# One encoder layer on one core: where the plan puts the last attention head's neighbours, and how the last block of the final layer norm is cut up

## The chip, the cores and the metric

The kernel runs on one core of a Trainium2 chip. The metric is device time in microseconds (us) of one execution. A core has five engines with a queue each, which run in order and wait for each other through semaphores: TensorE (PE; its weight loads are shown as PEld), VectorE (DVE), ScalarE (ACT), GpSimd (POOL) and SyncE (SP). SP issues most DMAs; GpSimd issues those that add to what lies in the destination.

## The reference

One post-norm encoder layer over 512 tokens of width 1024, all in float32:

```python
proj = h @ w_in[l]                                   # q, k, v of both mixers
o_a = windowed_gqa_sink(qa, ka, va, a_sink[l])       # 16 q heads, 4 kv heads, |i-j| <= 128
o_b = dilated_mixture(qb, kb, vb)                    # 4 head slots, three dilations each
gates = jax.nn.sigmoid(h @ w_gate[l] + b_gate[l])
g_a, g_b = jnp.split(gates, N_BRANCH, axis=-1)
mixed = g_a * (o_a @ w_br_a[l]) + g_b * (o_b @ w_br_b[l])
y = mixed @ w_out[l]
h = layer_norm(DN_ALPHA * h + y, ln1_g[l], ln1_b[l])
f = (jax.nn.silu(h @ w_ff_gate[l]) * (h @ w_ff_up[l])) @ w_ff_down[l]
h = layer_norm(DN_ALPHA * h + f, ln2_g[l], ln2_b[l])
```

The layer norm takes mean and variance over the 1024 columns of a token, divides by sqrt(var + 1e-5), multiplies by a vector g and adds a vector b.

## The kernel before

**Products.** Every float32 operand is split into a high part (a copy rounded to fp32r) and a low part (the rest), and a product is three matmuls: high by high, high by low, low by high. So each weight tile of 128 x 512 (256 KB) costs a DMA, a copy on ScalarE or VectorE (L368, L370) and a subtraction on VectorE (`tt`, L539, or `split`, L394) before TensorE can use it. A 512-column matmul reads its columns in pairs (c, c + 256), so the 512 columns of a PSUM bank stand interleaved (`pairs`, `back`).

**The plan.** The program is not written in the order in which it runs. Each step adds operations to a list with `op`: its engine and estimated time, what it reads and writes, and a priority, which is the TensorE time of the plan so far plus an offset. `Program.run` then plays the list through with estimated times and issues, for each engine whenever it is free, the ready operation of the lowest priority. The real order of every queue comes out of this play. Limits stand for memory: `ws` staging tiles for loaded weights, `whl` tiles for their high and low parts, `gen` general tiles (`N_GEN` of them), `oa` tiles for fetched attention outputs. For a DMA the play adds up a common transfer time `moved` (1.0 times the cost of the DMA after the start) and lets it land 2.4 us later.

**ORDER.** The first half is a written list of steps. `P:a,b` computes two products of x at once with fewer multiplications (`pair_x`: seven products of 12 matmuls with 256 columns, L634 to L636; weights `A11`, `S1`, `A12`, `S3`, `A22`, of which `S1` and `S3` are each a load and a summing load on top). `g` is one gate's product alone (`gate`, `feat_k`, L518 to L520, 24 matmuls with 512 columns). `A0` to `A3` are the four windowed attention heads' groups (`unit_a`: scores L865 and L866, exponentials L1021, transposes L968, value products L1034 and L1035), `B0` to `B3` the dilated ones (`unit_b`, exponentials L1103). `R` turns rows (L707, L718, L806 are its copies from tile to tile by DMA), `V12` are two value projections (`token_values`, L939 to L941; eight tiles of weights, 96 matmuls of 512 columns), `L` lowers the limits from `N_WSA`, `N_WHLA` = 8, 16 to `N_WS`, `N_WHL` = 6, 12 once the last pair in front of it is done (`env["mark"]`). `O` fetches an attention output for the branch products (`fetch_oa`): a plain DMA (L1302) and a summing one from GpSimd (L1303), then a split (L1288). Gates of pairs are put away in DRAM (L1224) and fetched later.

**The final block.** `tok_major` ends both layer norms' products. In the second call (`fine` true), for each block of 128 tokens t, two PSUM banks `acc[t, 0]` and `acc[t, 1]` hold the two 512-column halves; for t = 2 and 3 the residual was copied into the banks first (`into`), so nothing need be added. For t = 3, the last, the work runs: the matmuls of half 0, its statistics (L1514), the matmuls of half 1, its statistics, their aggregation (L1517) to mean and variance, ScalarE's square root (L1519), (x - mean) * g on VectorE for each half (L1527), the reciprocal (L1530), and y * r + b on VectorE for half 0 whole and half 1 in two pieces of 256 columns (L1538), each followed by its store (`finish`, L1932).

Of the kernel before, what the change touches and what calls it, by code (L numbers as in the profile page):

```python
# [15 lines left out]
P = 128  # L16
# [44 lines left out]
UNITS = 2  # L61
SLOW = 340
SPIN = 4

CUTS = ((0, 128), (128, 256), (256, 512))
FIRST = {("k", 0): (-1000, -998.2, -997.2), ("q", 0): (-998.8, -998.1, -997.1), ("v", 0): (-998.7, -998, -997),
# [3 lines left out]
N_ALONG, N_WHL0 = 2, 24  # L70
ALONG_CUTS = ((0, 256), (256, 512))
FIRST.update({(0, 0): (-997.45, -996.97), (0, 1): (-996.65,), (1, 0): (-997.4, -996.96), (1, 1): (-996.45,)})
N_WS, N_WHL, N_ATT, N_GEN = 6, 12, 16, 60

# [4 lines left out]


ORDER = """
VA q1 A0 q2 q3 g X P:k1,q4 R A1 P:q5,g P:q6,q7 R A2 P:g,g A3 P:g,g P:Q00,K00 R P:Q01,K01 R L g V12 Q02 K02 R V0 B0 Q10 K10 R Q11 K11 R B1 O O Q12 K12 R O O B2 B3 O O O O g7
"""
FORMS = -60.0
XT_AFTER, LN_AFTER = ("B", 2), "b4"
STORE, OA, OA_SPLIT, OB_SPLIT, N_OA, N_XA = 0.0, -60.0, -140.0, -140, 4, 4
PACK = -60.0
BY_DMA = ()  # L90
AWAY = range(8, 16)
# [37 lines left out]
class Program:  # L129
# [67 lines left out]
    def run(self):  # L197
# [26 lines left out]
        while n_left:  # L224
# [11 lines left out]
            while progress:  # L236
                progress = False
                for e in engines:
# [26 lines left out]
                    o.eng = e  # L265
                    if e == SP:
                        end = now + (0.62 if 14 < now < SLOW else 0.47)
                        moved = max(moved, now + 0.9) + (1.5 if now < 9.5 else 1.0 if now < SLOW else 0.92) * cost
                        o.done = moved + (2.4 if 14 < now < SLOW else 0.87)
                    elif o.moves:  # L270
                        end = now + cost
                        moved = max(moved, end + 0.3) + (1.0 if 14 < now < SLOW else 0.92) * o.moves
                        o.done = moved + (0.87 if e == ACT else 6.2 if 330 < now < 420 else 3.2 if 14 < now < SLOW else 2.2)
                    else:
                        end = now + cost
                        o.done = end
# [50 lines left out]
def hybrid_layer(ctx: ExitStack, tc: tile.TileContext, wpack, xT, xtok, sink, bgate,  # L327
# [543 lines left out]
    def turned_values(u, nt, turn_by=0, done=None):  # L871

        src = []
        w = S // nt
        for i in range(2):
            ps = done
            if i or not done:
                ps = bank("dense")
                feat_x(ps, unit(u + i))
            t = slot()  # L880

            def evac(e, t=t, ps=ps):
# [9 lines left out]
            op(cp_alts(S, True, 0.3 if turn_by else 0.1)[:2 if turn_by else 1], evac, reads=[ps], writes=[t], prio=EV if i else NORM)  # L892
# [403 lines left out]
    def fetch_oa(k):  # L1296
# [5 lines left out]
        op([(SP, 0.73)], lambda e: nc.sync.dma_start(st.t, src(0)), reads=got, writes=[st], prio=OA)  # L1302
# [144 lines left out]
    xt = {(t, j): slot() for t in range(NR) for j in range(2)}  # L1447
    for t in range(NR):
        for j in range(2):
            load(xt[t, j], xtok[t, :, j * S:(j + 1) * S], after=env[XT_AFTER], prio=-30)  # L1450

    def ln_vectors(gsrc, bsrc, after):
        res = []
# [7 lines left out]
    def tok_major(nk, last, us_of, u0, g, b, finish, fine, alpha=ALPHA, between=None, into=(0, 1, 2), gates=()):  # L1461
# [4 lines left out]
        pr.hold = True  # L1466

        def kmm(k, t, j, c0, c1, us, wu):
            wh, wl = wu[j]
            ps = acc[t, j]  # L1470

            def go(e):
                a0, a1 = us[0].t[:, t * P:(t + 1) * P], us[1].t[:, t * P:(t + 1) * P]
                o = ps.t[:, c0:c1]
                mm(o, a0, pairs(wh.t[:, c0:c1]), start=(k == 0 and t not in into), stop=False, skip_group_check=True)  # L1475
                mm(o, a0, pairs(wl.t[:, c0:c1]), start=False, stop=False, skip_group_check=True)  # L1476
                mm(o, a1, pairs(wh.t[:, c0:c1]), start=False, stop=(k == nk - 1), skip_group_check=True)  # L1477
# [19 lines left out]
        for t in range(NR):  # L1497
            if not gates and t in into:
                preload(t)
            st = stats()  # L1500
            pieces = [(0, 0, S), (1, 0, S)]
            toks = []
            N2 = NORM - 10 * (fine and t == NR - 1)
            for n, (j, c0, c1) in enumerate(pieces):
                ps, z = acc[t, j], xt[t, j]
                for k, us, wu in res:
                    kmm(k, t, j, c0, c1, us, wu)
                toks.append(z)
# [5 lines left out]
                op([(DVE, dve(S))], lambda e, y=y, st=st, n=n: nc.vector.bn_stats(  # L1514
                    st.t[:, 6 * n:6 * n + 6], y.t), reads=[y], writes=[(st, n)], prio=N2)
            np_ = len(pieces)
            op([(DVE, 0.1)], lambda e, st=st, np_=np_: nc.vector.bn_aggr(st.t[:, 32:34], st.t[:, 0:6 * np_]),  # L1517
               reads=[(st, n) for n in range(np_)], writes=[(st, "a")], prio=N2)
            op([(ACT, 0.2)], lambda e, st=st: nc.scalar.activation(  # L1519
                st.t[:, 34:35], st.t[:, 33:34], AF.Sqrt, bias=eps.t[:, 0:1]), reads=[(st, "a"), eps],  # L1520
               writes=[(st, "s")], prio=N2, table="r")
            for (j, c0, c1), tok in zip(pieces, toks):
# [3 lines left out]
                op([(DVE, dve(S, extra=0.06))], lambda e, z=z, y=y, st=st, j=j, view_=view_:  # L1526
                   nc.vector.scalar_tensor_tensor(  # L1527
                       halves(z.t), view_(y.t), st.t[:, 32:33], halves(g[j].t), op0=ALU.subtract,
                       op1=ALU.mult), reads=[tok, y, (st, "a"), g[j]], writes=[tok], prio=N2)
            op([(DVE, 0.08)], lambda e, st=st: nc.vector.reciprocal(st.t[:, 35:36], st.t[:, 34:35]),  # L1530
               reads=[(st, "s")], writes=[(st, "r")], prio=N2)
            if fine and t == NR - 1:
                pieces = [(0, 0, S), (1, 0, S // 2), (1, S // 2, S)]
                toks = [xt[t, 0], (xt[t, 1], 0), (xt[t, 1], 1)]
            for (j, c0, c1), tok in zip(pieces, toks):
                z = xt[t, j]
                op([(DVE, dve(c1 - c0, extra=0.06))], lambda e, z=z, st=st, j=j, c0=c0, c1=c1:
                   nc.vector.scalar_tensor_tensor(  # L1538
                       z.t[:, c0:c1], z.t[:, c0:c1], st.t[:, 35:36], b[j].t[:, c0:c1], op0=ALU.mult,
                       op1=ALU.add), reads=[z, (st, "r"), b[j]], writes=[tok], prio=N2)  # L1540
                finish(t, j, c0, c1, tok)
            if between:
                between(t)
        pr.hold = False
# [496 lines left out]
```

## Time and profile before

| what | value |
|---|---|
| three runs | 730.40, 731.12, 732.73 us; median 731.12 |
| the profiled execution | 732.24 us, of which the span of the profile is 730.5 us |
| granted TensorE clock | 0.998 |
| TensorE busy | 719.8 us (99%) |
| VectorE, ScalarE, GpSimd busy | 656.0, 466.8, 136.8 us |
| DMA | 139.5 MB, mean 191 GB/s |

A group's row gives line, engine, operation, tiles (out<-in), shape and count, then busy us and the mean ns of one, then the idle time of the engine just before them and what ended it. A row of the time line gives start and duration in us; matmuls overlap in the pipeline, so the step from start to start, not the duration, is what one costs.

### The profile page before, as it was taken

Reading aid. Unit: us, or ns where it says so; the run is one execution under the profiler, and the core shown is the slowest. Engines: PE = TensorE matmul, PEld = TensorE weight load, DVE = VectorE, ACT = ScalarE, POOL = GpSimd, SP = SyncE. Lnnn points to the kernel's source line nnn. Section 1 sums busy time; section 2 is a strip of 40 time slices with the busy share of each in tenths; the row PEclk is TensorE's granted clock in tenths of the full one; section 3 lists DMA queues with packets and bytes.
Section 4 is the critical chain, followed back from the end, with each engine's and each line's share of the span. In section 5 each row is a group of like instructions: output and inputs, shape, how many; then the busy total and the mean of one; then the engine's idle time right before and its main releaser. Section 6 shows DMA issues by size and latency. Waiting matters only on the chain.

```text
span 730.5 us, 14312 instructions
## 1 busy us (share of the span) xinstructions
PE 719.8 (99%) x4731; PEld 665.6 (91%) x4731; DVE 656.0 (90%) x1404; ACT 466.8 (64%) x1069; POOL 136.8 (19%) x295
## 2 busy tenths in 40 slices
PE   9999999999999999999999999999999999999995
PEld 7889999898898888988888999999999999999984
DVE  6999999888888798898987999799999999899987
ACT  5667787777787575765451666656666556666821
POOL 0021211111010641530020021111102111113000
PEclk9999999999999999999999999999999999999999
DMA  8878789966759487765792389676888888979402
GB/s 262 286 162 204 178 231 238 276 173 170 191 142 227 130 214 209 243 186 173 214 208 68 97 270 226 160 185 155 210 247 214 204 200 225 257 190 198 100 30 86
DMA packets 87578, 139.51 MB, mean 191 GB/s; under 512 B 11088, under 2 KB 24016, under 8 KB 87504
## 3 DMA queue, kind: packets, MB, share of 16 engines
q1 hardware_dynamic: 74192, 114.61, 51.9%
q0 software_dynamic: 13040, 23.86, 20.2%
q8 instruction: 37, 0.61, 0.3%
q14 instruction: 37, 0.30, 0.1%
q10 hardware_dynamic: 272, 0.13, 0.1%
HBM read 114.18 MB, written 7.60 MB: 167 GB/s over the span
## 4 chain that ended last, share of the span: by engine, by line
PE 89%; DMA 6%; DVE 2%; SPq 2%; ACT 1%; issue 1%; DVEq 0%; ACTq 0%
PE ps L1686 9%; PE ps L1685 9%; PE ps L1687 9%; PE ps L518 7%; PE ps L519 7%; PE ps L520 7%; PE ps L1896 4%; PE ps L1898 4%; PE ps L1897 4%; PE ps L1476 3%; PE ps L1475 3%; PE ps L1477 3%; PE ps L968 3%; DMA sl<-wpack 2%; PE ps L634 2%; PE ps L636 2%
## 5 line engine op out<-in xcount | busy, mean ns | idle before, releaser
L368 ACT ACTIVATE sl<-sl 128x512 fp32r<-128x512 f32 (+3 forms) x413 | 226.3, 582 | 45.0 <-DVE sl L539 21.9
L539 DVE TENSOR_TENSOR sl<-sl,sl 128x512 fp32r<-128x512 f32 (+3 forms) x369 | 216.3, 622 | 6.5 <-ACT sl L368 2.9
L368 ACT ACTIVATE sl<-ps 128x256 f32<-128x256 f32 (+6 forms) x211 | 88.9, 443 | 92.0 <-PE ps L1687 56.8
L382 POOL DMA_DIRECT2D sl<-wpack x58 | 51.0, 879 | 345.0 <-DMA sl<-wpack 79.6
L518 PE MATMUL ps<-x,sl 128*128 128x512 f32 (+1 forms) x257 | 99.4, 387 | 0.1
L520 PE MATMUL ps<-x,sl 128*128 128x512 f32 (+1 forms) x257 | 97.3, 379 | 0.0
L1686 PE MATMUL ps<-sl,sl 128*128 128x256 f32 x352 | 96.8, 275 | 0.0
L1687 PE MATMUL ps<-sl,sl 128*128 128x256 f32 x352 | 96.8, 275 | 0.0
L1685 PE MATMUL ps<-sl,sl 128*128 128x256 f32 x352 | 96.8, 275 | 0.0
L519 PE MATMUL ps<-x,sl 128*128 128x512 f32 (+1 forms) x225 | 85.4, 380 | 0.0
L1685 PE MATMUL ps<-x,sl 128*128 128x256 f32 x264 | 72.6, 275 | 0.0
L1686 PE MATMUL ps<-x,sl 128*128 128x256 f32 x264 | 72.6, 275 | 0.0
L1687 PE MATMUL ps<-x,sl 128*128 128x256 f32 x264 | 72.6, 275 | 0.0
L394 DVE TENSOR_TENSOR sl<-sl,sl 128x512 fp32r<-128x512 f32 x98 | 65.6, 685 | 2.9 <-ACT sl L368 1.3
L1685 PEld LDWEIGHTS ps<-sl,sl 128*128 128x128 f32 x352 | 67.6, 192 | 0.1
L1686 PEld LDWEIGHTS ps<-sl,sl 128*128 128x128 f32 x352 | 67.6, 192 | 0.1
L1687 PEld LDWEIGHTS ps<-sl,sl 128*128 128x128 f32 x352 | 67.6, 192 | 0.0
L520 PEld LDWEIGHTS ps<-x,sl 128*128 128x128 f32 x257 | 48.8, 190 | 6.8
L518 PEld LDWEIGHTS ps<-x,sl 128*128 128x128 f32 x257 | 48.9, 190 | 6.1 <-ACT x L368 0.5
L1686 PEld LDWEIGHTS ps<-x,sl 128*128 128x128 f32 x264 | 50.6, 192 | 0.4
L1685 PEld LDWEIGHTS ps<-x,sl 128*128 128x128 f32 x264 | 50.6, 192 | 0.4
L1687 PEld LDWEIGHTS ps<-x,sl 128*128 128x128 f32 x264 | 50.7, 192 | 0.0
(174 smaller groups left out, 1818.1 us busy)
## 6 DMA issues: line engine op xcount, KB each, us to landing
sl<-wpack SPq DMA_DIRECT2D x248, 256.0 KB, 4.1
sl<-wpack POOLq DMA_DIRECT2D x58, 256.0 KB, 5.4
sl<-sl SPq DMA_DIRECT2D x110, 128.0 KB, 4.0
wf<-wpack SPq DMA_DIRECT2D x51, 256.0 KB, 5.1
wf<-wpack POOLq DMA_DIRECT2D x24, 256.0 KB, 6.3
oa<-sl SPq DMA_DIRECT2D x32, 128.0 KB, 3.7
sl<-sl SPq DMA_DIRECT2D x68, 32.0 KB, 2.4
sl<-oa SPq DMA_DIRECT2D x8, 256.0 KB, 3.9
```

The lines of the kernel that those rows point to most:

```text
L368: nc.scalar.activation(dst, src, AF.Copy)
L382: op([(POOL, 1.0)], lambda e: nc.gpsimd.dma_start(b.t, src2, accum_op=ALU.add), reads=[b], writes=[b], prio=prio, moves=1.65)
L394: op([(DVE, dve(S))], lambda e: nc.vector.tensor_tensor(l.t, src.t, f32(h.t), op=ALU.subtract), reads=[src, h], writes=[l], prio=prio, abs ...
L518: mm(o, a, x0, start=(k == 0 and begins), stop=False, skip_group_check=split)
L519: mm(o, a, x1, start=False, stop=False, skip_group_check=split)
L520: mm(o, b, x0, start=False, stop=(k == nk - 1), skip_group_check=split)
L539: op([(DVE, dve(w))], lambda e: nc.vector.tensor_tensor(dst(), x(), y(), op=o), reads=reads, writes=writes, prio=prio)
L1685: mm(o, wh, pairs(bh[k]()), start=(first and k == 0), stop=False, skip_group_check=True)
L1686: mm(o, wh, pairs(bl[k]()), start=False, stop=False, skip_group_check=True)
L1687: mm(o, wl, pairs(bh[k]()), start=False, stop=(k == 3), skip_group_check=True)
L1896: mm(ps.t, x0, pairs(w[0].t), start=(first and m == 0), stop=False, skip_group_check=True)
L1897: mm(ps.t, x0, pairs(w[1].t), start=False, stop=False, skip_group_check=True)
```

## The change

In `ORDER` the plain gate `g` that stood after `L` moves to directly behind `A3`, in front of the gate pair `P:g,g`; `L` moves from behind the pair `P:Q01,K01` to in front of the pair `P:Q00,K00`; and `V12` moves from behind both of these pairs to between them. In the play, a DMA between 90 and 165 us takes `RATE` = 1.7 times its cost, and `N_GEN` becomes 62. Each `fetch_oa` may be issued only after the exponentials of `B1` (and all before them). `LATE`, `VAL`, `XT_AFTER` and `OB_SPLIT` are new names or forms for values that stay the same.

In the final block of 128 tokens, half 1 is computed in two pieces of 256 PSUM columns, each with all its matmuls (24 of 256 columns for 12 of 512), and statistics are taken in four pieces of 256. Because of the interleaving, PSUM's first 256 columns are not the output's first 256; the second normalising step reads every other column. Output columns 256 to 511 of half 1 are normalised by ScalarE (x * r - mean * r, with a new small product on VectorE for mean * r), and multiplied by g and increased by b on GpSimd; VectorE does the rest. There are four stores of 256 columns, and the one behind GpSimd is the last.

```diff
+LATE = 2.4
+RATE = 1.7
...
-N_WS, N_WHL, N_ATT, N_GEN = 6, 12, 16, 60
+N_WS, N_WHL, N_ATT, N_GEN = 6, 12, 16, 62
...
-VA q1 A0 q2 q3 g X P:k1,q4 R A1 P:q5,g P:q6,q7 R A2 P:g,g A3 P:g,g P:Q00,K00 R P:Q01,K01 R L g V12 Q02 K02 R V0 B0 Q10 K10 R Q11 K11 R B1 O O Q12 K12 R O O B2 B3 O O O O g7
+VA q1 A0 q2 q3 g X P:k1,q4 R A1 P:q5,g P:q6,q7 R A2 P:g,g A3 g P:g,g L P:Q00,K00 R V12 P:Q01,K01 R Q02 K02 R V0 B0 Q10 K10 R Q11 K11 R B1 O O Q12 K12 R O O B2 B3 O O O O g7
...
-XT_AFTER, LN_AFTER = ("B", 2), "b4"
-STORE, OA, OA_SPLIT, OB_SPLIT, N_OA, N_XA = 0.0, -60.0, -140.0, -140, 4, 4
+SPREAD = True
+VAL = -100.0
+OA_AFTER = (1, 1, 1, 1, 1, 1, 1, 1)
+XT_AFTER, LN_AFTER = [('B', 2), ('B', 2), ('B', 2), ('B', 2)], "b4"
+STORE, OA, OA_SPLIT, OB_SPLIT, N_OA, N_XA = 0.0, -60.0, -140.0, -140.0, 4, 4
...
-                        moved = max(moved, now + 0.9) + (1.5 if now < 9.5 else 1.0 if now < SLOW else 0.92) * cost
-                        o.done = moved + (2.4 if 14 < now < SLOW else 0.87)
+                        moved = max(moved, now + 0.9) + (1.5 if now < 9.5 else RATE if 90 < now < 165 else 1.0 if now < SLOW else 0.92) * cost
+                        o.done = moved + (LATE if 95 < now < 150 else 2.4 if 14 < now < SLOW else 0.87)
...
-        op([(SP, 0.73)], lambda e: nc.sync.dma_start(st.t, src(0)), reads=got, writes=[st], prio=OA)
+        op([(SP, 0.73)], lambda e: nc.sync.dma_start(st.t, src(0)), reads=got, writes=[st], prio=OA, after=env["B", OA_AFTER[k]])
...
+            cut = c1 - c0 < S
...
-                mm(o, a0, pairs(wh.t[:, c0:c1]), start=(k == 0 and t not in into), stop=False, skip_group_check=True)
-                mm(o, a0, pairs(wl.t[:, c0:c1]), start=False, stop=False, skip_group_check=True)
-                mm(o, a1, pairs(wh.t[:, c0:c1]), start=False, stop=(k == nk - 1), skip_group_check=True)
-
-            op([(PE, 3 * pe(c1 - c0))], go, reads=[us[0].tok, us[1], wh, wl], writes=[ps])
+                w0, w1 = (pairs(w.t)[:, c0 // 2:c1 // 2] for w in (wh, wl))
+                mm(o, a0, w0, start=(k == 0 and t not in into), stop=False, skip_group_check=True)
+                mm(o, a0, w1, start=False, stop=False, skip_group_check=True)
+                mm(o, a1, w0, start=False, stop=(k == nk - 1), skip_group_check=True)
+
+            op([(PE, 3 * pe(c1 - c0))], go, reads=[us[0].tok, us[1], wh, wl] + ([ps] if cut else []),
+               writes=[(ps, c0) if cut else ps])
...
-            pieces = [(0, 0, S), (1, 0, S)]
+            ends = fine and t == NR - 1
+            pieces = [(0, 0, S // 2), (0, S // 2, S), (1, 0, S // 2), (1, S // 2, S)] if ends else [(0, 0, S), (1, 0, S)]
...
-                for k, us, wu in res:
-                    kmm(k, t, j, c0, c1, us, wu)
-                toks.append(z)
+                cut = (ps, c0) if ends and j else ps
+                if j or not ends:
+                    for k, us, wu in res:
+                        kmm(k, t, j, c0, c1, us, wu)
+                elif n == 0:
+                    for k, us, wu in res:
+                        kmm(k, t, j, 0, S, us, wu)
+                if c0 == 0:
+                    toks.append(z)
...
+                if ends and j and SPREAD:
+                    op([(DVE, dve(S // 2, extra=0.06))], lambda e, z=z, y=y, st=st, j=j: nc.vector.scalar_tensor_tensor(
+                        z.t[:, 0:256], back(y.t)[:, 0], st.t[:, 32:33], g[j].t[:, 0:256], op0=ALU.subtract,
+                        op1=ALU.mult), reads=[tok, (y, 0), (st, "a"), g[j]], writes=[(tok, 0)], prio=N2)
+                    continue
...
+                    z, ps, c = xt[t, 1], acc[t, 1], slice(S // 2, S)
+                    op([(DVE, 0.08)], lambda e, st=st: nc.vector.scalar_tensor_tensor(
+                        st.t[:, 36:37], st.t[:, 32:33], -1.0, st.t[:, 35:36], op0=ALU.mult, op1=ALU.mult),
+                       reads=[(st, "a"), (st, "r")], writes=[(st, "m")], prio=N2)
+                    op([(ACT, act(S // 2))], lambda e, st=st, z=z, ps=ps, c=c: nc.scalar.activation(
+                        z.t[:, c], back(ps.t)[:, 1], AF.Identity, scale=st.t[:, 35:36], bias=st.t[:, 36:37]),
+                       reads=[(st, "m"), ps, z], writes=[toks[2]], prio=N2)
+                    for x, o in ((g, ALU.mult), (b, ALU.add)):
+                        op([(POOL, 0.5)], lambda e, z=z, x=x, o=o, c=c: nc.gpsimd.tensor_tensor(
+                            z.t[:, c], z.t[:, c], x[1].t[:, c], op=o), reads=[toks[2], x[1]], writes=[toks[2]], prio=N2)
+                    pieces = [(1, 0, S // 2), (0, 0, S // 2), (0, S // 2, S)]
+                    toks = [toks[1], (xt[t, 0], 0), (xt[t, 0], 1), toks[2]]
...
+            if ends and SPREAD:
+                finish(t, 1, S // 2, S, toks[3])
```

More of the change, by code (lines that the diff above doesn't have):

```diff
@@ L890, in evac @@
                         copy(e, d, s)
-            op(cp_alts(S, True, 0.3 if turn_by else 0.1)[:2 if turn_by else 1], evac, reads=[ps], writes=[t], prio=EV if i else NORM)
+            op(cp_alts(S, True, 0.3 if turn_by else 0.1)[:2 if turn_by else 1], evac, reads=[ps], writes=[t], prio=VAL if i else NORM)
             src.append(t)
@@ L1449, in hybrid_layer @@
         for j in range(2):
-            load(xt[t, j], xtok[t, :, j * S:(j + 1) * S], after=env[XT_AFTER], prio=-30)
+            load(xt[t, j], xtok[t, :, j * S:(j + 1) * S], after=env[XT_AFTER[t]], prio=-30)
     def ln_vectors(gsrc, bsrc, after):
@@ L1513, in tok_major @@
                 y = z if t not in into else ps
-                op([(DVE, dve(S))], lambda e, y=y, st=st, n=n: nc.vector.bn_stats(
-                    st.t[:, 6 * n:6 * n + 6], y.t), reads=[y], writes=[(st, n)], prio=N2)
+                op([(DVE, dve(c1 - c0))], lambda e, y=y, st=st, n=n, c0=c0, c1=c1: nc.vector.bn_stats(
+                    st.t[:, 6 * n:6 * n + 6], y.t[:, c0:c1]), reads=[cut if t in into else y], writes=[(st, n)], prio=N2)
             np_ = len(pieces)
@@ L1521, in tok_major @@
                writes=[(st, "s")], prio=N2, table="r")
-            for (j, c0, c1), tok in zip(pieces, toks):
+            for j, tok in enumerate(toks):
                 z, ps = xt[t, j], acc[t, j]
                 y = z if t not in into else ps
+                if ends and j and SPREAD:
[3 more added lines that the diff above has]
+                    continue
                 view_ = halves if t not in into else back
@@ L1528, in tok_major @@
                        halves(z.t), view_(y.t), st.t[:, 32:33], halves(g[j].t), op0=ALU.subtract,
-                       op1=ALU.mult), reads=[tok, y, (st, "a"), g[j]], writes=[tok], prio=N2)
+                       op1=ALU.mult), reads=[tok, y, (st, "a"), g[j]], writes=[tok], prio=N2 + (ends and SPREAD and 1))
             op([(DVE, 0.08)], lambda e, st=st: nc.vector.reciprocal(st.t[:, 35:36], st.t[:, 34:35]),
                reads=[(st, "s")], writes=[(st, "r")], prio=N2)
-            if fine and t == NR - 1:
+            pieces = [(0, 0, S), (1, 0, S)]
+            if ends:
                 pieces = [(0, 0, S), (1, 0, S // 2), (1, S // 2, S)]
                 toks = [xt[t, 0], (xt[t, 1], 0), (xt[t, 1], 1)]
+                if SPREAD:
+                    z, ps, c = xt[t, 1], acc[t, 1], slice(S // 2, S)
[10 more added lines that the diff above has]
+                    toks = [toks[1], (xt[t, 0], 0), (xt[t, 0], 1), toks[2]]
             for (j, c0, c1), tok in zip(pieces, toks):
@@ L1539, in tok_major @@
                        z.t[:, c0:c1], z.t[:, c0:c1], st.t[:, 35:36], b[j].t[:, c0:c1], op0=ALU.mult,
-                       op1=ALU.add), reads=[z, (st, "r"), b[j]], writes=[tok], prio=N2)
+                       op1=ALU.add), reads=[z, tok, (st, "r"), b[j]], writes=[tok], prio=N2)
                 finish(t, j, c0, c1, tok)
+            if ends and SPREAD:
+                finish(t, 1, S // 2, S, toks[3])
             if between:
```

## The prediction

> **What bounds the kernel now.** I read the page first, then the busy time by stretches of 20 us, then TensorE's groups and the waits in the one stretch that stands out, then the time line of the end.
>
> ```profile
> PE 719.8 (99%) x4731; PEld 665.6 (91%) x4731; DVE 656.0 (90%) x1404; ACT 466.8 (64%) x1069; POOL 136.8 (19%) x295
> ```
>
> TensorE is busy for 719.8 of 730.5 us. So nothing can be gained by speeding another engine up, only where TensorE stands still. The stretches say where that is (the columns are the window, its length, busy us of PE, PEld, DVE, ACT and POOL with their instructions, the clock, the DMA share and GB/s):
>
> ```profile
> 120.00:140.00 20.00, 18.37 (x147) 16.98 (x145) 16.45 (x40) 14.79 (x39) 2.90 (x9) 1.00 0.99 283
> ...
> 160.00:180.00 20.00, 20.00 (x111) 18.01 (x110) 16.81 (x49) 15.42 (x41) 2.83 (x9) 1.00 0.66 177
> ...
> 420.00:440.00 20.00, 20.00 (x182) 20.00 (x181) 19.43 (x38) 13.77 (x28) 4.98 (x6) 1.00 0.88 261
> ```
>
> In 120 to 140 us TensorE lacks 1.6 us by busy time, and at the same moment the 16 DMA engines are full (share 0.99). Twenty microseconds later the share is 0.66. But a matmul's row overlaps its neighbours, so busy time hides short stalls. Counting is stricter. The row at 420 us holds nothing but 256-column matmuls and fits 182 of them into 20.00 us: 0.11 us each at full pace. TensorE's groups within 120 to 140 us:
>
> ```profile
> L634 PE MATMUL ps<-sl,sl 128*128 128x256 f32 x21 | 5.9, 283 | 0.2 <-ACT sl L642 0.2
> L635 PE MATMUL ps<-sl,sl 128*128 128x256 f32 x20 | 5.5, 275 | 0.0
> L636 PE MATMUL ps<-sl,sl 128*128 128x256 f32 x20 | 5.5, 275 | 0.0
> L634 PE MATMUL ps<-x,sl 128*128 128x256 f32 x18 | 5.0, 279 | 0.0
> L635 PE MATMUL ps<-x,sl 128*128 128x256 f32 x18 | 5.0, 275 | 0.0
> L636 PE MATMUL ps<-x,sl 128*128 128x256 f32 x18 | 5.0, 275 | 0.0
> L968 PE MATMUL ps<-ident,sl 128*128 128x128 f32 x16 | 2.6, 287 | 0.2 <-ACT sl L956 0.2
> L865 PE MATMUL ps<-sl,sl 128*128 128x384 f32 x6 | 2.0, 328 | 0.0
> L866 PE MATMUL ps<-sl,sl 128*128 128x384 f32 x6 | 2.0, 326 | 0.0
> L1035 PE MATMUL ps<-sl,sl 128*128 128x512 f32 x2 | 1.0, 483 | 1.2 <-DVE sl L973 1.1
> L1034 PE MATMUL ps<-sl,sl 128*128 128x512 f32 x2 | 0.8, 382 | 0.0
> ```
>
> 115 matmuls of 256 columns and 16 transposes at 0.11 us are 14.4 us, the 12 of 384 columns at one and a half times that 2.0, the four of 512 at twice that 0.9: 17.2 us of work in 20 us. So **2.8 us are lost in this stretch**. The largest loss lies between these two:
>
> ```profile
> 132.76 0.38 PE L1034 MATMUL ps<-sl,sl 128*128 128x512 f32 x1
> 134.26 0.48 PE L1035 MATMUL ps<-sl,sl 128*128 128x512 f32 x1 [1.11 <-DVE sl L973]
> ```
>
> The second should start about 0.22 us after the first and starts 1.50 us after it. It is the second half of an attention head's value product, and waits for VectorE's low part of the probabilities. What VectorE and ScalarE waited for themselves in 120 to 142 us:
>
> ```profile
> ACT sl L368 <- DMA gz<-sl: 2.1, 1, 2.1
> ACT sl L368 <- DMA sl<-sl: 1.5, 1, 1.5
> ACT sl L642 <- DMA sl<-sl: 1.2, 1, 1.2
> ```
> ```profile
> DVE sl L539 <- DMA sl<-sl: 2.1, 2, 1.8
> ```
>
> So the stall is a queue's: a copy or a split stands at the head of ScalarE's or VectorE's queue, waiting for a transfer that the plan had expected earlier, and the attention head's work, ready, stands behind it.
>
> **The change part by part.** *The order and the plan's constants.* Nothing is added to TensorE here. A weight-saving pair is 84 matmuls of 256 columns, 84 x 0.11 = 9.2 us, and takes 7 tiles of 256 KB: 0.19 MB per us. A plain gate is 24 matmuls of 512 columns, 5.2 us for 2 tiles, and V12 is 96, 20.7 us for 8 tiles: 0.10 MB per us each. Before, the last four pairs stand in one row and the gate and V12 after them; now the gate goes in front of the second gate pair and V12 between the last two pairs, so the heavy stretch is broken twice by work that needs half as much. The plan's RATE makes transfers 1.7 times as long between 90 and 165 us, so work that needs one is put later in the queues of ScalarE and VectorE, behind attention work that is ready. Both act on exactly the wait above. The fetches of attention outputs also leave the stretch:
>
> ```profile
> L1302 SPq DMA_DIRECT2D sl<-oa x8: 357/400/544, 136.0 to 244.7; - x8
> ```
> ```profile
> 268.83 0.50 ACT L1103 ACTIVATE sl<-sl,st 128x256 f32<-128x256 f32 x1
> ```
> ```profile
> 310.17 0.38 PE L518 MATMUL ps<-sl,sl 128*128 128x512 f32 x1
> 310.38 0.38 PE L519 MATMUL ps<-sl,sl 128*128 128x512 f32 x1
> ```
> ```profile
> sl<-wpack SPq DMA_DIRECT2D x248, 256.0 KB, 4.1
> sl<-wpack POOLq DMA_DIRECT2D x58, 256.0 KB, 5.4
> ```
>
> The first two of the eight (the first at 136.0 us), each with a summing transfer on GpSimd's queue behind it, go at the crowded time. Now all eight stand behind the exponentials of the second dilated head, which end at about 269 us (second row). They move past everything that SP and GpSimd issue until then, and the summing ones come among GpSimd's exchange copies of the dilated heads. Four buffers make two rounds of 4.1 + 5.4 = 9.5 us, so they have landed by about 288 us. The branch products that need them start at 310 us (third rows): some 20 us of dense products hide the move, and I cost it at nothing. Were that cover gone, TensorE would wait up to one round, 9.5 us. The constants that repeat their old value (LATE, VAL, XT_AFTER, OB_SPLIT) cost nothing, and two more general tiles (N_GEN) only allow more. I take the stall as gone: **-2.8 us**, ends 0 and -2.8. The transfers named above are then next to come late, elsewhere in the same stage.
>
> *The final block.* The end now:
>
> ```profile
> 722.64 0.38 PE L1477 MATMUL ps<-sl,sl 128*128 128x512 f32 x1
> 723.06 0.70 DVE L1514 BATCH_NORM_STATS2 st<-ps 128x6 f32<-128x512 f32 x1 [0.68 <-PE ps L1477]
> 723.79 0.21 DVE L1517 BATCH_NORM_AGGREGATE st<-st 128x2 f32<-128x12 f32 x1
> 724.04 0.29 ACT L1519 ACTIVATE st<-st,eps 128x1 f32<-128x1 f32 x1 [4.89 <-DVE st L1517]
> 724.04 1.41 DVE L1527 SCALAR_TENSOR_TENSOR sl<-ps,st,sl 128x512 f32<-128x512 f32 x2
> 725.37 0.15 DVE L1530 RECIPROCAL st<-st 128x1 f32<-128x1 f32 x1
> 725.55 1.54 DVE L1538 SCALAR_TENSOR_TENSOR sl<-sl,st,sl 128x512 f32<-128x512 f32 x3
> ```
>
> From 723.02 to 727.09 us only VectorE works; then come the last store and 3.4 us up to the span's end, which stay. Back to back a 512-wide VectorE pass is 1.41 / 2 = 0.70 us and a 256-wide one (1.54 - 0.70) / 2 = 0.42.
> - TensorE: 24 matmuls of 256 columns for 12 of 512, 24 x 0.11 = 2.64 against 12 x 0.21 (the step between the two rows at 310 us) = 2.52: +0.1 us.
> - The last statistics cover 256 columns: -0.28 us. But the first piece's statistics read the PSUM bank that the second piece's matmuls write. In the plan VectorE is busy with the block before, so that read falls among the second piece's products. If it holds them, TensorE stands for one pass and two hand-overs of 0.04 us (723.02 to 723.06): 0.5 us. If other columns of a bank may be written meanwhile, it costs 0. The row nearest is L634's wait for ScalarE's evacuation of its bank in the groups above (0.2 us idle); it shows the hold, though for the same columns. I take +0.45 us, ends 0 and 0.6.
> - The Trainium skill, "PSUM — Partial Sum Buffer", section "PSUM bank collisions raise a hardware error", says that accesses should be guarded by bank and quadrant, not by address. By that rule the term would be 0.5 us, by a guard on columns 0; no row here shows two engines on one bank at different columns.
> - Normalising takes 724.04 to 727.09 = 3.05 us now. Afterwards VectorE does 0.42 + 0.70 + 0.10 (reciprocal, the part that shows) + 0.15 (the new mean-times-scale, as a reciprocal) = 1.37 us, then ScalarE's pass over 256 columns, then GpSimd's product and sum one after the other; VectorE's own three 256-wide passes end earlier. Prices:
>
> ```profile
> L956 ACT ACTIVATE sl<-sl,st 128x256 f32<-128x256 f32 x37 | 16.4, 496 | 1.7 <-DVE st L1024 1.5
> ```
> ```profile
> L1113 POOL COPY st<-st 32x2 f32<-32x2 f32 x64 | 19.0, 297 | 7.6 <-ACT sl L1079 5.1
> ```
> ```profile
> L1056 POOL MEMSET sl<- 128x64 f32 x4 | 0.6, 153 | 4.1 <-DMA sl<-sl 3.4 <-PE ps L1034 0.7
> ```
>
> ScalarE's nearest pass has one column operand and takes 0.50 us; with two I take 0.55. No row has GpSimd combine two tiles. A copy of next to nothing takes 0.30 us, and a write of 64 columns without an input 0.15, so at most 2.4 ns a column. The low end for 256 columns is 0.30 us, the copy's fixed part alone; the high end is 0.30 + 256 x 2.4 ns = 0.92. I take the middle, 0.6 us, for each of the two, and 0.04 us for each of three hand-overs. Sum: 1.37 + 0.55 + 1.2 + 0.12 = 3.24 us, +0.2 against now, ends -0.4 and +0.85.
> - The Trainium skill, "GPSIMD Engine Reference", section 3.1, gives 2.6 cycles per element at 1.2 GHz for a two-input product, so 0.55 us for 256 columns and, by an estimate, some 0.7 with the start of the instruction; this term would then be +0.4 us. No run so far shows it.
>
> The block together: 0.1 + 0.45 - 0.28 + 0.2 = **+0.5 us** (ends -0.6 and +1.3). Splitting the work does not shorten the end, because the new chain of three engines is as long as the one it replaces.
>
> **The sum.** The profiled execution took 732.24 us, 730.5 of them its span; it lies 1.1 us above the median of the runs, 731.12. 732.24 - 2.8 + 0.5 = 729.9 us on its scale, **728.8 us** on the scale of the median: 0.32% faster. Measurements of this kernel tell about 0.3%, 2.2 us, from no change, so the forecast stands just beyond that bound, and a third of the stall staying would bring it inside.
>
> **The rivals.**
> *The stall only shrinks or moves.* The bytes and transfers stay the same in number, and a plan that errs by a microsecond on one landing makes the next stall. For it: outside this stretch TensorE is full already, so a re-planned stage can only lose. Against it: the rows at 160 us show the DMA engines with a third of their time free a moment later, to be had for the taking. With half of the 2.8 us left, and 0.5 to 1.3 at the end: 731.1 - 1.4 + 0.5 (to 1.3) = 730.2 to 731.0 us, no change that can be told.
>
> *Slower: the weight buffers run short.* The step L now comes before the last two pairs, not after them. It cuts the staging tiles from 8 to 6 and the split ones from 16 to 12. A pair uses 5 staging tiles in 9.2 us, 1.85 us each, so six tiles look 11.1 us ahead and eight 14.8. Two of the five are summed by two transfers one behind the other, 4.1 + 5.4 = 9.5 us at the median over the kernel. At 9.5 they are in time. The rival decides from 11.1 us on, 17% above the median, which transfers in a full stage can pass. At 12.1 us each of four summed tiles comes 1.0 us late, and each drags 0.7 us of split on VectorE behind it (0.70 us for 512 columns): 4 x 1.7 = 6.8 us, less what attention fills, which I put at half: 3.4. If the head of the queue is held in this way the old stall stays as well: 731.1 + 3.4 + 0.5 = 735.0 us. For it: at 120 to 140 us the DMA share is 0.99. Against it: V12 now stands between the two pairs and takes half the bytes per us, and the plan with RATE at 1.7 assumes late landings.
>
> *The end costs more, or the change does less than it says.* If the order settles as forecast but the end takes +1.3 us, 729.6 us; if GpSimd is quick and the bank is not held, 727.7. If the plan that comes out has nearly the same queue order around 130 us, the stall is untouched and only the end counts: 731.6 us.
>
> **How the numbers follow.** The forecast (stall gone, the end up to somewhat dearer) gets 0.52 for being faster by over 0.3%: the waits name the mechanism, and three parts of the change act on it (the order, RATE, the later fetches). No change within 0.3% gets 0.20: the shrunken stall, the untouched plan, the dear end. Slower by over 0.3% gets 0.28: the buffers, and other losses in stages that are full now. The range runs from 727.5 (stall gone and the end quick) to 735.5 (just beyond the buffers' case, 735.0). The forecast's own range is 727.5 to 729.6.
>
> **What would show it.** Right: 120 to 140 us with TensorE at 20.00 us, no 1 us wait of L1035 for VectorE, DMA share below 0.95 there, the first fetch of the attention outputs after 260 us. At the end: a GpSimd product and sum of 256 columns as the last work, the last store about 0.5 us later after the last matmul's old place than now, and a gap among the second piece's matmuls of some 0.45 us if the bank is held. Wrong: TensorE waiting for ScalarE's or VectorE's splits in the last two pairs (buffers), or a new wait anywhere between 160 and 350 us, where there is none now; GpSimd's passes far from 0.6 us would spoil the end's sum.

## The result and the profile after

The changed kernel takes **734.58 us** (median of 6 runs, 733.65 to 735.53), the kernel before in the same session 731.02 us (729.5 to 732.73). The ratio is 1.0044, with a 95% interval of 1.0031 to 1.0056: slower by 3.2 us by this ratio (the two medians lie 3.6 us apart), beyond the 0.3% that can be told. The profiled execution took 735.53 us, 733.8 of them its span, which is 3.3 us longer than the span before. I had forecast 2.3 us less.

The page's first row, in which TensorE's busy time has hardly changed:

```profile
PE 719.9 (98%) x4743; PEld 666.3 (91%) x4743; DVE 654.8 (89%) x1403; ACT 470.1 (64%) x1074; POOL 137.3 (19%) x297
```

So the time came from places where TensorE stands, or from after its last matmul. Busy time by stretches of the changed kernel (same columns as before):

```profile
120.00:140.00 20.00, 20.00 (x166) 19.61 (x165) 18.47 (x43) 16.69 (x40) 1.86 (x8) 1.00 0.62 172
...
310.00:320.00 10.00, 8.96 (x37) 6.33 (x36) 5.60 (x17) 5.25 (x13) 8.76 (x35) 1.00 1.06 321
```

The old stall is gone: 166 matmuls where there were 147, the DMA share down from 0.99 to 0.62. Counted by starts, each against the usual step of a matmul of its shape, TensorE had lost 3.3 us between 120 and 160 us and now loses nothing there. But a new stall stands at 311 to 320 us. That count gives 2.7 us from 300 to 330 us, 2.4 of them in the stall itself, and nothing was lost there before. The waits of the changed kernel from 310 to 320 us (total us, times, longest):

```profile
ACT x L373 <- DMA sl<-oa: 4.3, 4, 2.1
DVE sl L1293 <- ACT x L373: 2.9, 3, 1.7
PEld ps L524 <- DVE sl L1293: 1.9, 4, 0.6
...
PE ps L524 <- DVE sl L1293: 0.6, 3, 0.2
```

This reads upwards from TensorE: the product waits for VectorE's low part, that for ScalarE's rounding, and that for a fetch of the attention outputs (`sl<-oa`), one of the transfers that the change made later. And the time line of the end:

```profile
721.10 0.28 PE L1485 MATMUL ps<-sl,sl 128*128 128x256 f32 x1
721.42 0.43 DVE L1530 BATCH_NORM_STATS2 st<-ps 128x6 f32<-128x256 f32 x1
...
721.90 0.38 PE L1483 MATMUL ps<-sl,sl 128*128 128x256 f32 x1 [0.53 <-DVE st L1530]
...
722.88 0.43 DVE L1530 BATCH_NORM_STATS2 st<-ps 128x6 f32<-128x256 f32 x1 [1.03 <-PE ps L1485]
723.34 0.26 DVE L1533 BATCH_NORM_AGGREGATE st<-st 128x2 f32<-128x24 f32 x1
...
723.64 0.48 DVE L1542 SCALAR_TENSOR_TENSOR sl<-ps,st,sl 128x256 f32<-128x256 f32 x1
724.04 0.74 DVE L1548 SCALAR_TENSOR_TENSOR sl<-ps,st,sl 128x512 f32<-128x512 f32 x1
724.70 0.15 DVE L1551 RECIPROCAL st<-st 128x1 f32<-128x1 f32 x1
724.89 0.16 DVE L1560 SCALAR_TENSOR_TENSOR st<-st 128x1 f32<-128x1 f32 x1
...
725.14 0.56 ACT L1563 ACTIVATE sl<-ps,st 128x256 f32<-128x256 f32 x1 [1.21 <-DVE st L1560]
725.86 1.76 POOL L1567 TENSOR_TENSOR sl<-sl,sl 128x256 f32<-128x256 f32 x2 [39.12 <-ACT sl L1563]
```

GpSimd's two passes end at 727.62 us, and 6.1 us later the span, where 3.4 had followed the last VectorE pass before. The chain that ended last says with what it closes (start, us, what):

```profile
725.86 0.96 POOL sl L1567
726.82 0.04 issue
726.86 0.76 POOLq L2074
```

L2074 is the end of the program. Every engine closes its queue there with an instruction called a drain, and then all of them meet in a barrier, that is, each waits until the others have come. The source view of that line after, then of the same line (L2036) before; the columns are shortest, median and longest in ns, then the first and last start in us:

```profile
L2074 POOLq EVENT_SEMAPHORE  x4: 17/17/17, 733.0 to 733.7; - x4
L2074 POOLq DRAIN  x3: 51/93/6107, 726.9 to 733.5; - x3
L2074 SPq DRAIN  x3: 7/7/7, 729.9 to 733.2; - x3
```

The same line before:

```profile
L2036 POOLq EVENT_SEMAPHORE  x4: 17/17/17, 729.7 to 730.4; - x4
L2036 POOLq DRAIN  x3: 51/102/9037, 686.6 to 730.2; - x3
L2036 SPq DRAIN  x3: 7/7/13, 729.6 to 729.9; - x3
```

After, GpSimd's first drain starts with its last pass, at 726.86 us, and lasts 6.11 us, to 732.97, which is 5.35 us behind the pass's end. SyncE has seen all stores land at 729.9 us, and the barrier's first step waits until 733.0. Before, GpSimd's drain lay at 686.6 to 695.6 us, where nobody waited for it; the barrier followed SyncE by 0.1 us.

### The profile page after: what moved, and what is told of

It is laid out like the page before. It is cut to its first block, busy times and chain, and to the rows that moved or that the text cites. A ratio compares the mean times of both kernels' runs of the same rounds, so it can differ in the third digit from the quotient of the medians.

```text
span 733.8 us, 14304 instructions
## 1 busy us (share of the span) xinstructions
PE 719.9 (98%) x4743; PEld 666.3 (91%) x4743; DVE 654.8 (89%) x1403; ACT 470.1 (64%) x1074; POOL 137.3 (19%) x297
## 4 chain that ended last, share of the span: by engine, by line
PE 91%; DMA 4%; POOL 1%; SPq 1%; DVE 1%; issue 0%; ACT 0%; POOLq 0%; ACTq 0%
PE ps L1724 9%; PE ps L1723 9%; PE ps L1725 9%; PE ps L524 7%; PE ps L523 7%; PE ps L525 7%; PE ps L1934 4%; PE ps L1936 4%; PE ps L1935 4%; DMA sl<-wpack 4%; PE ps L641 3%; PE ps L640 3%; PE ps L639 3%; PE ps L1483 3%; PE ps L973 3%; PE ps L1485 3%
## 5 line engine op out<-in xcount | busy, mean ns | idle before, releaser
L373 ACT ACTIVATE sl<-ps 128x256 f32<-128x256 f32 (+5 forms) x210 | 88.5, 441 | 93.3 <-PE ps L1725 56.9
```

Source lines behind the costliest of these rows:

```text
L373: nc.scalar.activation(dst, src, AF.Copy)
```

## The experiments

The theory after this comparison: the new end costs mostly GpSimd's closing drain, 3.05 us between SyncE at 729.96 and GpSimd at 733.01, and the late fetches moved the loss of 120 us to 311 us. The rivals put the cost of the end on work: on the longer chain of three engines with the bank that is held, or on a drain whose length goes with what GpSimd did. For the fetches the rival was that the loss at 311 us comes with the new order whatever the fetches do.

**The final block without GpSimd's part** (e1): the changed kernel with one constant turned.

```diff
-SPREAD = True
+SPREAD = False
```

> The changed kernel with its new order and its two matmul pieces, but with the last normalising done by VectorE alone: ScalarE and GpSimd do nothing there. Theory A (GpSimd's own closing step costs the time: in the changed kernel SyncE is through at 729.96 us, and all engines wait until 733.01 us for the drain that follows GpSimd's last pass): the 3.05 us go, and the work on the way to the last store gets about 0.8 us shorter, so about 3.8 us below the changed kernel, 730.8 us on the scale where the kernel before takes 731.0. Theory B (the new order is what costs, the end only a few tenths): 734 us or more.

Measured: 730.45 us, ratio 0.998 (0.9972 to 0.9989). GpSimd's drain is back under the work, and the wait of the second piece's products for the first piece's statistics stays. The part on GpSimd and ScalarE costs 1.0044 - 0.998 = 0.0064 of the time, some 4.7 us.

**The change without its final block, and the final block without the rest** (e2, e3):

```diff
 e2: changed kernel, with tok_major() of before
 e3: kernel before, with tok_major() of the change and SPREAD = True
```

> The new order, constants and late fetches, with the final block of the kernel before. Theory A: the stall at 120 to 140 us stays gone (-3.0 us, and -0.4 behind it), the new one at 311 to 319 us stays (+2.7 us), the end is the old one: 0.5 to 1.0 us below the kernel before, so 730.0 to 730.5 us, no drain behind SyncE's last step. Theory B: 734 us.

> The order of the kernel before with the new final block. Theory A: the end brings 3.05 us of drain, 0.7 us in which TensorE is held by the first piece's statistics and 0.5 us of longer work: 3.5 to 4.5 us above the kernel before, 734.5 to 735.5 us, more than the changed kernel itself. Theory B: at most 1 us above, 732 us.

Measured: e2 729.93 us, ratio **0.9975** (0.9964 to 0.9986); e3 736.3 us, ratio 1.0061 (1.0048 to 1.0074). So the plan's part of the change gains 1.8 us and the final block costs 4.5 us on the old plan. In e2 TensorE still loses 2.3 us by the count from 300 to 330 us, so that loss belongs to the plan's part. In e3 the drain again ends 5.35 us behind GpSimd's last pass.

**One idle copy on GpSimd** (e4): before, plus an instruction that moves 128 values nobody reads.

```diff
+LAST_TOUCH = NR - 1
...
+            if fine and t == LAST_TOUCH:
+                op([(POOL, 0.3)], lambda e, st=st: nc.gpsimd.tensor_copy(st.t[:, 40:41], st.t[:, 35:36]),
+                   reads=[(st, "r")], writes=[(st, "t")], prio=N2)
```

> The kernel before with one more instruction: behind the last block's reciprocal GpSimd copies one column of 128 values, which nothing reads. It is off every path, so a theory that counts work expects no change (731.0 us). Theory A with a drain of fixed length behind any last GpSimd instruction (5.35 us after the end of the pass in the changed kernel): the copy ends near 725.9 us, the drain near 731.3, while SyncE is through at 729.7, so 1.3 to 1.8 us more, 732.3 to 732.8 us. If the drain is long only behind a wide two-input pass, no change.

Measured: 733.63 us, ratio 1.0026 (1.0016 to 1.0037). The copy in the time line, and the end of the program in the source view:

```profile
724.78 0.70 POOL L1534 COPY st<-st 128x1 f32<-128x1 f32 x1 [37.85 <-DVE st L1531]
```
```profile
L2040 POOLq EVENT_SEMAPHORE  x4: 17/17/17, 730.9 to 731.5; - x4
L2040 POOLq DRAIN  x3: 51/93/6057, 724.8 to 731.3; - x3
L2040 SPq DRAIN  x3: 7/7/7, 728.8 to 731.1; - x3
```

The copy takes 0.70 us and its drain 6.06, to 730.83: 5.35 us behind the copy's end, as behind the two passes over 256 columns. SyncE is through at 728.83 us, so 2.0 us are open, and 1.9 us is what the runs show. Between these two sizes the work that GpSimd did doesn't matter, only when it did the last of it. A theory that prices the work itself falls on this.

**The same copy one block earlier** (e10): `LAST_TOUCH = NR - 2`.

> Before plus one copy of 128x1 on GpSimd, as in the run where the copy came after the last block's reciprocal, but after the reciprocal of the block before the last; nothing reads it. Theory A (GpSimd's closing drain ends 5.35 us after its last pass and counts only from the point at which it passes the last store's landing): the copy ends near 721 us, the drain near 726.5, SyncE goes on to about 729, so the time is that of before, ratio 1.000. Rival B (a late GpSimd instruction costs its 2 us by being there, whether or not the store still covers it): ratio 1.0026 as in that run.

Measured: 731.35 us, ratio 0.9998 (0.9986 to 1.001). Time line and source view:

```profile
718.89 0.70 POOL L1534 COPY st<-st 128x1 f32<-128x1 f32 x1 [32.67 <-DVE st L1531]
```
```profile
L2040 POOLq DRAIN  x3: 51/102/6058, 718.9 to 728.6; - x3
L2040 SPq DRAIN  x3: 7/7/7, 728.0 to 728.3; - x3
```

The drain is as long as in e4 but ends at 724.9 us, before SyncE's first at 728.0, and costs nothing. The copy ended 1.4 us earlier than I had put it (719.6 for 721 us), so the cover is 3.1 us for the 2.5 that I had expected.

**The parts of the plan, one by one, on the kernel before** (e6 the order line, e7 RATE, e8 the late fetches):

```diff
 e6
-... R A2 P:g,g A3 P:g,g P:Q00,K00 R P:Q01,K01 R L g V12 Q02 K02 R V0 ...
+... R A2 P:g,g A3 g P:g,g L P:Q00,K00 R V12 P:Q01,K01 R Q02 K02 R V0 ...
 e7
-... 1.0 if now < SLOW else 0.92) * cost
+... 1.7 if 90 < now < 165 else 1.0 if now < SLOW else 0.92) * cost
 e8
-... prio=OA)
+... prio=OA, after=env["B", 1])
```

> The kernel before with the new ORDER line alone (the gate in front of the second gate pair, L in front of the last two pairs, V12 between them). If the mixing of heavy and light stretches is what removed the 2.8 us stall: ratio 0.996, no wait over 0.3 us at 120 to 140 us. If the plan needs RATE to see the transfers as late: the stall stays or moves, ratio 0.998 to 1.002.

> The kernel before with RATE 1.7 alone (the plan takes transfers between 90 and 165 us as 1.7 times as long). If late-landing transfers at the head of a queue were the whole cause: ratio 0.996. If the four pairs in a row simply ask for more than the DMA engines give: TensorE still waits at 120 to 160 us, ratio 0.999 or above.

> The kernel before with the late fetches of attention outputs alone. The first of them went at 136 us, after most of the old stall, so the old stall stays within 1 us, and the new one near 310 us comes: 2 to 3 us more, ratio 1.003 to 1.004. Rival (the fetches helped make the old stall): ratio 1.000 or below.

Measured: e6 730.22 us, ratio 0.9981 (0.997 to 0.9991); e7 734.72 us, 1.0043 (1.003 to 1.0056); e8 737.1 us, 1.0066 (1.0054 to 1.0078). Some of the values that e7 and e8 compute differ from the reference's (relative error 0.24 in both), and the cause was not traced. They run all 4731 matmuls, and I use them only for the places of the stalls. Busy time by stretches of e6, e7 and e8, the last with two rows:

```profile
120.00:140.00 20.00, 20.00 (x168) 19.56 (x167) 18.84 (x43) 16.38 (x39) 2.49 (x6) 1.00 0.84 233
```
```profile
120.00:140.00 20.00, 18.02 (x146) 16.83 (x145) 17.60 (x37) 15.65 (x34) 1.61 (x7) 1.00 0.83 213
```
```profile
120.00:140.00 20.00, 19.00 (x155) 18.10 (x154) 17.45 (x41) 16.27 (x40) 2.96 (x9) 1.00 0.98 273
...
320.00:340.00 20.00, 18.61 (x94) 15.12 (x93) 17.89 (x47) 12.02 (x29) 8.07 (x35) 1.00 0.64 208
```

The order alone fills the old stall (168 matmuls), with the DMA engines still at 0.84. But it loses 2.3 us in smaller pieces between 320 and 400 us, the largest 1.0 us just before 400, and it reaches only 0.9981, not the 0.996 expected of it: the stall partly moved. RATE alone doesn't fill the stall (146), and loses another 1.7 us at 400 to 420. The late fetches alone leave 1.8 us of its 3.3, so the early fetches had a share in it, which I had not expected; but they lose 5.3 us between 314 and 353, more than the 2 to 3 expected. So the order is enough to remove the stall, and RATE and the fetches, each alone, are no gain; for these two that rests on kernels whose values are partly wrong. The parts don't add up, since each makes the plan set out every queue anew.

**The order and RATE without the late fetches** (e5): e2 with `after=env["B", OA_AFTER[k]]` taken out.

> New order and constants, old final block, and the attention outputs may be fetched as soon as they are written, as in the kernel before. Theory (the late fetches make the new stall at 311 to 319 us; their second round of four was issued only at 298.8 us and landed at 311 to 317.5): that stall's 2.3 to 2.7 us go, and if order and RATE alone keep 120 to 140 us free, the ratio to the kernel before is 0.9975 - 0.0033 = 0.994. Rival (the early fetches are part of what crowds 120 to 160 us): the stall there comes back by 1 us or more, ratio 0.996 or above.

Measured: 737.19 us, ratio 1.0072 (1.006 to 1.0084), so that my expectation of 0.994 failed. The loss at 311 us is gone (0.03 us by the same count from 300 to 320), as the theory says. The old stall does not come back either, although two fetches go at 131 us again, so the rival's mechanism fails too. But 8.7 us are lost at 178 to 192. Stretches, the second of them inside the first, and the waits there:

```profile
180.00:200.00 20.00, 16.20 (x102) 14.36 (x102) 15.60 (x40) 13.01 (x35) 1.51 (x8) 0.83 0.84 209
...
185.40:192.20 6.80, 5.43 (x22) 4.48 (x21) 3.25 (x8) 3.82 (x10) 0.00 (x0) 0.50 1.07 248
```
```profile
PEld ps L1040 <- DVE sl L978: 2.8, 2, 1.7
PEld ps L1039 <- ACT sl L373: 2.3, 2, 1.2
PE ps L1040 <- DVE sl L978: 2.0, 2, 1.4
```

Not all of the loss is waiting. From 185.4 to 192.2 us the granted clock is 0.50 (second row, the column before the DMA share), and the matmuls after the last wait, from 187.8 us on, take twice their usual step: 2.2 of the 8.7 us.

The third and fourth fetch go at 172.7 and 173.2 us, and the sums behind them at 177.5 and 178.2; the moves between heads (L811) that follow at 180.8 us land 5.5 us after their issue, where the changed kernel has 2.2. With this order and RATE the late fetches do protect something: without them 8.7 us are lost at 180 us, with them 2.3 at 311 us. That these transfers hold up the moves is read from the order of the queue and was not tried by itself.

**Taking the second round of fetches out of the way** (e11, e12): e2 with six buffers, and e2 with the fetches let go and ranked earlier.

```diff
 e11
-... OA_SPLIT, OB_SPLIT, N_OA, N_XA = 0.0, -60.0, -140.0, -140.0, 4, 4
+... OA_SPLIT, OB_SPLIT, N_OA, N_XA = 0.0, -60.0, -140.0, -140.0, 6, 4
 e12
-OA_AFTER = (1, 1, 1, 1, 1, 1, 1, 1)
+OA_AFTER = (0,)*8
...
-... OA, OA_SPLIT, OB_SPLIT, N_OA, N_XA = 0.0, -60.0, -140.0, -140.0, 4, 4
+... OA, OA_SPLIT, OB_SPLIT, N_OA, N_XA = 0.0, -100.0, -140.0, -140.0, 4, 4
```

> The kernel with the change's order, constants and late fetches and the old final block (0.9975 of before), with six buffers for the fetched attention outputs, not four; six of the eight fetches then stand together in SyncE's queue and only two wait for the splits of the first. Theory A (the 2.3 us lost at 311 to 319 us come from the second round, which four buffers hold back until 299 us): with two fetches left in it, half of the loss or less stays, 728.8 to 728.0 us, ratio 0.9960 to 0.9950. Rival B (the DMA engines, at a share of 1.07 there, set when they land, not the buffers): the loss stays or moves to the weights behind them, ratio 0.9975 or more.

> The same kernel with four buffers, the fetches let go after the first dilated head, not the second, and ranked 40 us earlier in the plan: two of them come 20 places earlier in SyncE's queue, the last two 11 places earlier. Theory A (they only have to land before 311 us): the loss at 311 to 319 us goes, no other comes, 727.6 us, ratio 0.9945. Rival B (any earlier place takes DMA time from something else, as the fetches without a wait did at 178 to 189 us): a new loss of 1 to 5 us between 220 and 300 us, ratio 0.9975 to 1.003.

Measured: e11 735.68 us, ratio 1.0057 (1.0038 to 1.0076); e12 738.22 us, 1.009 (1.0073 to 1.0107). Both are slower than e2, by 0.8% and 1.2%. In e11 the loss at 311 us falls from 2.3 to 1.5 us; in e12, whose fetches have all landed by 305.2 us, it is gone. But e11 loses 5.4 us at 347 to 355 us, and e12 3.8 us at 280 to 288 and 6.0 at 350 to 358. The 3.8 us are what the rival of e12 had foreseen; no expectation had the losses at 350 us. The stretches of e2 and then of e11:

```profile
320.00:345.00 25.00, 25.00 (x147) 22.45 (x146) 23.73 (x56) 17.11 (x42) 6.05 (x24) 1.00 0.55 177
345.00:355.00 10.00, 10.00 (x48) 8.74 (x47) 10.00 (x17) 6.91 (x13) 0.00 (x0) 1.00 0.61 193
```
```profile
320.00:345.00 25.00, 25.00 (x145) 22.40 (x144) 22.46 (x58) 14.18 (x33) 5.48 (x19) 1.00 0.42 139
345.00:355.00 10.00, 6.90 (x26) 5.27 (x25) 8.67 (x19) 6.08 (x12) 0.00 (x0) 0.83 0.79 260
...
351.30:354.80 3.50, 3.50 (x9) 2.77 (x10) 2.50 (x4) 2.96 (x6) 0.00 (x0) 0.51 0.63 205
```

In e2 VectorE is full from 345 to 355 us (10.00 of 10). In e11 it did 1.3 us less and ScalarE 2.9 us less in the 25 us before, and TensorE waits for a copy of ScalarE's at 347 us. That this is the work left undone is my reading and was not tested. Here too a part of the loss is clock and not waiting: behind the waits of 3.9 us the granted clock is 0.51 from 351.3 to 354.8 us (last row), which costs another 1.5 us, and in e12 it is 0.50 from 354.7 to 358.1 us, 1.6 of the 6.0 us. So the mechanism at 311 us is as the theory has it (the second round's landing), but neither way of taking the fetches earlier was free. Why the plan puts splits off in e11 wasn't followed further.

**The best version** of these is e2, the change with the old final block: 729.93 us at 0.9975 of before. The order line alone (e6, 0.9981) can't be told from it. Both intervals lie below 1, but the gain, 1.4 to 1.8 us, is less than the 0.3% that I called tellable.

## Why the prediction failed

The spans differ by +3.3 us, and I had -2.3. By the steps of the sum, each in the profiled executions:

| step | taken | measured |
|---|---|---|
| stall at 120 to 160 us | -2.8 | -3.3 |
| late fetches | 0 | +2.7 |
| 24 matmuls of 256 columns for 12 of 512 | +0.1 | +0.1 |
| hold of the second piece's products | +0.45 | +0.7 |
| last statistics | -0.28 | -0.27 |
| aggregate | 0 | +0.05 |
| normalising | +0.2 | +0.93 |
| last pass to the end of the span | 0 | +2.7 |
| the rest, not assigned | 0 | -0.3 |

**Right: the stall.** It went, and e6 shows that the order alone is enough for that. All signs that I had asked for are there: 20.00 us busy, no wait of 1 us for the value product, DMA share below 0.95, the first fetch after 260 us (277.4). Of the three parts that I said act on it, RATE alone did nothing there. My sum for 120 to 140 us has a slip: the groups add up to 17.3 us, not 17.2, so 2.7 were lost and not 2.8. Counted by starts it is 3.0 us there and 0.4 in the 20 us behind.

**Wrong: "3.4 us up to the span's end, which stay".** This step cost 2.7 us, as much as the fetches below, and it is the one that the experiments settle best. I costed the work that GpSimd was given and not the instruction that ends its queue. The row was in the profile: L2036's drain of 9.04 us, from 686.6 us, ended 34 us before the barrier. With a GpSimd pass ending at 727.62 us the cover was gone. In e4 and e10 an instruction of 128 values has a drain of the same length, and it costs time only when it is late. The point from which it counts follows: GpSimd's last pass plus 5.35 us against SyncE's end. In the kernel before SyncE's first drain is at 729.6 us, so GpSimd had to be done by about 724.3 us. VectorE has the last block's mean at 724.0 there, so a GpSimd pass behind ScalarE's could not have met that.

**Wrong: the late fetches at nothing.** I let two rounds of 9.5 us start at 269 us and end at 288, before the branch products at 310. The source view of both lines in the changed kernel:

```profile
L1307 SPq DMA_DIRECT2D sl<-oa x8: 319/384/545, 277.4 to 301.4; - x8
...
DMA to landing us min/median/max: 5.0/5.3/6.2
```
```profile
L1308 POOL DMA_DIRECT2D sl<-oa x8: 872/883/1109, 283.1 to 308.2; - x8
...
DMA to landing us min/median/max: 6.2/7.9/9.9
```

Three things were too short. The first round starts at 277.4 us, 12 us after the last exponential that lets it go (265.1 us), behind what SyncE has queued. A round takes not 4.1 + 5.4 but 5.3 + 7.9 = 13.2 us by the medians, in a stretch whose DMA share is 1.03 to 1.08; I had used the medians of weight transfers over the whole kernel. And the second round doesn't follow on the first: the first's sums land at 289.2 to 294.4 us, the second's first fetch goes at 298.8, and its sums land at 311.5, 313.5, 315.5 and 317.5, each at the moment at which one of ScalarE's four waits ends. So the cover of 20 us that I had put at nothing was used up. I had named the price with the cover gone, up to 9.5 us; it was 2.7.

**Mis-sized: the hold.** It is there, at 0.7 us against 0.45. The products stand from 721.21 to 721.90. I had counted the pass over the first piece and two hand-overs. What I left out is that the statistics can only begin when the piece's last matmul is through, and by the time line that is 0.28 us after its start (721.10 to 721.38), 0.17 more than the step of 0.11. With 0.04 to VectorE, 0.43 for the pass and 0.05 back, that is the 0.7. The pass reads columns that the held products don't write. The rule that the prediction quoted from the Trainium skill ("PSUM — Partial Sum Buffer", section "PSUM bank collisions raise a hardware error"), to guard by bank and quadrant and not by address, asks for such a guard, and the 0.5 that I worked out for it was nearer than my 0.45. The wait is one for a semaphore; what the chip does without it wasn't tried.

**Mis-sized: normalising.** It takes 723.64 to 727.62 = 3.98 us, where I had 3.24 and a high end of 3.9. GpSimd's passes are 0.96 and 0.72 us against 0.6 each, which is 0.5 of the 0.7; the hand-overs make up most of the rest (0.09 to ScalarE, 0.16 to GpSimd, 0.08 between its passes, against 0.04 each). By the estimate in the prediction from the Trainium skill's 2.6 cycles per element ("GPSIMD Engine Reference", section 3.1) it was 0.55 us, some 0.7 with the start; the second pass, at 0.72, agrees, and the first, at 0.96, does not.

**The rivals.** None was what happened. The slower one named the buffers of the weights after L, and its sign, splits late in the last two pairs, is not in the trace. "The stall moves" was right in kind, but I priced it as half of the stall left, 730.2 to 731.0 us, and in its old place. The measured time lies below my high end of 735.5 us by luck: that end stood for the buffers, which did nothing of the kind. The sign that I had named, a new wait between 160 and 350 us, did come.

## What to carry to other kernels

Before you give a last step to an engine that was idle, look up when that engine's closing drain ran and what covered it: its end, not the step's, decides. Price a transfer that you move by the landing times and the DMA share of the stretch into which it goes, and a second round by when the first one's buffers come free. And where a plan sets out all queues anew, expect a loss to move: here all three tries to clear 311 us (e5, e11, e12) brought a larger one at 180, 280 or 350 us.

## What was not expected of the hardware

GpSimd's drain at the end of the program ended 5.35 us after its last pass in four kernels (the changed one, e3, e4 and e10), whether that was a copy of 128x1 (0.70 us) or a sum over 128x256 (0.72 us); in the kernel before, where a GpSimd DMA issue was its last work, it ended 7.8 us after that. What the drain waits for in that time no run shows. Of the two passes over 128x256 the product took 0.96 us, after 39 us without work, and the sum directly behind it 0.72. In e5, e11 and e12 the granted TensorE clock fell to half for 3.4 to 6.8 us in or just behind a stall; e2, whose loss at 311 us comes in waits of some 0.5 us, kept the full clock there. And the landing time of one kind of move of 128 KB was 5.5 us in e5, where two fetches and two sums of 256 KB had been issued just ahead of it, and 2.2 in the changed kernel.
